# Decode-state streams issued from GpSimd's queue, up to three sequences ahead, in 14 buffers

## The chip, the cores and the metric

The kernel runs on one core of a Trainium2 chip. The metric is device time in microseconds, from runs without a profiler; the median of three is quoted. One further execution was taken with the hardware profiler, and every row below comes from that one.

## The reference, cut to what matters

One inference step of a one-layer decoder trunk, for 512 prompt tokens and, beside them, 8 decode sequences of one token each. In order: a mixer (RG-LRU heads and four mLSTM heads on one input projection), cross-attention of four heads over 256 memory tokens, and a squared-ReLU MLP; each is added to the residual. All arithmetic is fp32.

The decode sequences carry states of their own, and these are what the change is about:

```
# mLSTM, per decode sequence b and head h; C0[b,h] is 256 x 256
C_new = g_state * C + g_in * outer(v, k)          # written out as s_mlstm_C
num   = C_new @ q                                  # then divided by a denominator
# cross-attention, per decode sequence b and head h
s = q . K[b, :, h, :] * 512**-0.5                  # K: 256 memory tokens x 512
p = softmax(s)
o = p @ V[b, :, h, :]                              # V: 256 memory tokens x 512
```

K and V for 8 sequences and 4 heads are 16.8 MB each, C is 8.4 MB. Each is read once, so each is a stream from HBM.

## The kernel before, in words

Activations lie with features on the 128 partitions and 520 columns (512 prompt tokens and 8 decode tokens). A fp32 product is three matmuls: weight and activation are each split into a rounded high part and a low remainder. The whole kernel is one list of jobs. A job is a 512 KB granule of weights: it is loaded into one of three `wraw` buffers (`w_raw`, L103 to 106), split by ScalarE (`whi`, L121) and VectorE (`wlo`, L122), and multiplied on TensorE. `run_jobs` (L140) issues, for job i, the load of job i+3, the split of job i+2, the matmuls of job i, and its eviction. Loads and splits get a priority that moves them 100 instructions forward.

Everything that isn't a weight matmul is a task, a Python generator. `step_tasks` (L129) advances the open tasks once per job (`rate` and `cost` say how many steps), so that a task's instructions are interleaved with the jobs' on the in-order queues of the engines. A task started with a rate takes rate times cost steps a job: `attn_decode_all` has rate 2 (`DRATE`); a job of the projections `w_cq` has cost 1, a job of `w_mk` or `w_mv` cost 0.35 (`MCOST`).

Two tasks stream the decode states.

- `ml_decode(h)` (L442 to 503), once for each of the four mLSTM heads, in the stretch of the input projection. It writes q and k of the 8 sequences to a DRAM tile `dqk`, and then takes four steps of two sequences. A step needs two rows of `dqk`, each broadcast to 128 partitions (256 KB as written to SBUF, L475), and two granules of C (256 KB each, L479). ScalarE scales C (L493), VectorE adds the outer product (L494) and reduces against q (L497), and the new C is stored (L500).
- `attn_decode(h)` (L766 to 821), once a head, in the stretch of the projections `w_cq`, `w_mk` and `w_mv`. Eight steps of one sequence each load a broadcast row of q (L780, 256 KB) and two granules of K (L782, 256 KB each); VectorE multiplies and reduces (L792). After four empty steps come a TensorE transpose (L798), a softmax over 8 rows, and a store of the probabilities to a DRAM tile `dp` (L802). Eight more steps load a broadcast row of p (L806, 128 KB) and two granules of V (L808, 256 KB each), and VectorE reduces four times (L819).

`attn_prompt(h)` waits, as a task, until `attn_decode(h)` is done, before it multiplies by the values.

All DMAs are issued by one queue, SyncE's (`load = nc.sync.dma_start`), in the order that the job list and the tasks give them. That queue is in order: a load that waits for its buffer holds back whatever stands behind it. In the streams, a step starts the loads of the next step, so they run one step ahead. The buffers for K, V and all broadcast rows are one ring of six 2 KB tiles a partition (tag `kv`); granules of C lie in the general pool of 66 slots. GpSimd itself does 15 additions in the prologue, eight small memsets (L551) and 10 multiplications at the end.

Of the kernel before, what the change touches and what calls it, by code (L numbers as in the profile page):

```python
# [9 lines left out]
F32 = mybir.dt.float32  # L10
F32R = mybir.dt.float32r
AF = mybir.ActivationFunctionType
ALU = mybir.AluOpType
# [4 lines left out]
P = 128  # L18
TP = 512
NB = 8  # L20
# [6 lines left out]
NMEM = 256  # L27
# [18 lines left out]
def tile_trunk(ctx: ExitStack, tc: tile.TileContext, a, o):  # L46
    nc = tc.nc
    V, S, PE, G = nc.vector, nc.scalar, nc.tensor, nc.gpsimd
# [8 lines left out]
    small = early_pools.enter_context(tc.tile_pool(name="small", bufs=2))  # L57
# [6 lines left out]
    def nm(s):  # L64
        uid[0] += 1
        return f"{s}_{uid[0]}"

    def slot(name, shape=(P, T), dt=F32):
        return slots.tile(list(shape), dt, tag="slot", name=nm(name))

    def sm(name, shape, bufs=2, dt=F32):
        return small.tile(list(shape), dt, tag=name, name=nm(name), bufs=bufs)

    def stream(shape):
        return small.tile(list(shape), F32, tag="kv", name=nm("kv"), bufs=6)

    def aux():
        return late.get("aux", paux).tile([P, 512], F32, tag="aux", name=nm("aux"))
# [10 lines left out]
    def rows_of(d, off, n):  # L89
        return bass.AP(tensor=d.tensor, offset=d.offset + off, ap=[[0, P], [1, n]])  # L90

    load = nc.sync.dma_start
    HALF = [slice(0, HT), slice(HT, T)]
    DEC = slice(TP, T)
    CH = 128
# [64 lines left out]
    def gemm(srcs, acts, evac, pre=None, cols=(0, 1)):  # L160
# [4 lines left out]
        def mm(g, wh, wl):  # L165
# [3 lines left out]
            for j in range(8):  # L169
                k = g * 8 + j  # L170
                xh, xl = acts[k]
                for wi, (w, x) in enumerate(((wh, xh), (wh, xl), (wl, xh))):
                    for hf in cols:
                        PE.matmul(ps[:, hf, 0:HT], w[:, j, :], x[:, HALF[hf]],  # L174
                                  start=(k == 0 and wi == 0), stop=(k == n - 1 and wi == 2))
# [11 lines left out]
    def pc(base, i=0):  # L187
        return par[:, base + i:base + i + 1]
# [31 lines left out]
    def rstd_of(ssq, n, name):  # L220
        r = slot(name)
        v = slot(name + "v")
        for c in HALF:
            ps = aux()
# [217 lines left out]
    def ml_decode(h, q, k, hh):  # L442

        v = vv[h]
        qkd = sm("qkd", (NB, 512))
        tp = aux()
        for i, s_ in enumerate((q[0], q[1], k[0], k[1])):
            PE.transpose(out=tp[0:NB, i * P:(i + 1) * P], in_=s_[:, DEC], identity=ident)
        S.copy(qkd, tp[0:NB, :])
        dqk = dram.tile([NB, 512], F32, name=nm("dqk"))  # L450
        load(dqk, qkd)
        gv, t1, t2 = sm("gv", (P, 2, NB)), sm("t1", (P, 2, NB)), sm("t2", (P, 2, NB))
        for j in range(2):
            V.tensor_tensor(out=gv[:, j], in0=v[j][:, DEC], in1=bc[:, h, 1], op=ALU.mult)
            V.tensor_tensor(out=t1[:, j], in0=nst[:, h, j], in1=bc[:, h, 0], op=ALU.mult)
            V.tensor_tensor(out=t2[:, j], in0=k[j][:, DEC], in1=bc[:, h, 1], op=ALU.mult)
        V.tensor_tensor(out=t1, in0=t1, in1=t2, op=ALU.add)
        for j in range(2):
            V.tensor_tensor(out=t2[:, j], in0=t1[:, j], in1=q[j][:, DEC], op=ALU.mult)
        yield  # L460
        yield
        load(o["s_n"][:, h], t1)
        dps = aux()
        for j in range(2):
            PE.matmul(dps[:, 0:NB], ones, t2[:, j], start=(j == 0), stop=(j == 1))
        den, numd = sm("den", (P, NB)), sm("numd", (P, 2, NB))
        S.activation(den, dps[:, 0:NB], AF.Abs)
        V.tensor_tensor(out=den, in0=den, in1=bc[:, h, 2], op=ALU.max)
        V.reciprocal(den, den)

        def fetch(b2):
            qb, ct = [], []
            for b in (2 * b2, 2 * b2 + 1):
                t = stream((P, 512))
                load(t, rows_of(dqk, b * 512, 512))  # L475
                qb.append(t)
            for j in range(2):
                t = slot("ct", (P, 2, 256))
                load(t, a["C0"][h, j, :, 2 * b2:2 * b2 + 2])  # L479
                ct.append(t)  # L480
            return qb, ct

        cur = fetch(0)
        for b2 in range(NB // 2):
            yield
            qb, ct = cur
            if b2 + 1 < NB // 2:
                cur = fetch(b2 + 1)
            for j in range(2):
                for i in range(2):  # L490
                    b = 2 * b2 + i
                    c = ct[j][:, i]
                    S.activation(c, c, AF.Copy, scale=bc[:, h, 0, b:b + 1])  # L493
                    V.scalar_tensor_tensor(out=c, in0=qb[i][:, 256:512], scalar=gv[:, j, b:b + 1],  # L494
                                           in1=c, op0=ALU.mult, op1=ALU.add)
                    junk = sm("junk", (P, 256), 1)
                    V.tensor_tensor_reduce(out=junk, in0=c, in1=qb[i][:, 0:256], op0=ALU.mult,  # L497
                                           op1=ALU.add, scale=1.0, scalar=0.0,
                                           accum_out=numd[:, j, b:b + 1])
                load(o["s_C"][h, j, :, 2 * b2:2 * b2 + 2], ct[j])  # L500
        for j in range(2):
            V.tensor_tensor(out=hh[j][:, DEC], in0=numd[:, j], in1=den, op=ALU.mult)
        dec_done[h] = True

    def ml_prompt(h):
# [12 lines left out]
        for i in range(2):  # L518
            out = [slot("qk") for _ in range(2)]
            for j in range(2):  # L520
                for c in HALF:
                    ps = aux()
# [114 lines left out]
    def rnn(i, xc):  # L637
# [5 lines left out]
        for g in range(2):  # L643
            t = slot("g")
            for c in HALF:
                ps2 = aux()
# [104 lines left out]
    def softmax(ps, rows, out):  # L751
        mx = sm("mx", (P, 1), 4)[0:rows]
        su = sm("su", (P, 1), 4)[0:rows]
        V.reduce_max(out=mx, in_=ps, axis=AX.X)
        V.tensor_scalar(out=mx, in0=mx, scalar1=-SC, scalar2=None, op0=ALU.mult)
        S.activation(out, ps, AF.Exp, bias=mx, scale=SC, accum_out=su)
        V.reciprocal(su, su)
        V.tensor_scalar(out=out, in0=out, scalar1=su, scalar2=None, op0=ALU.mult)
# [7 lines left out]
    def attn_decode(h):  # L766
        q = qx[h]
        yield
        tp = aux()
        for j in range(4):  # L770
            PE.transpose(out=tp[0:NB, j * P:(j + 1) * P], in_=q[j][:, DEC], identity=ident)
        qd = sm("qkd", (NB, 512))
        S.copy(qd, tp[0:NB, :])
        dq = dram.tile([NB, 512], F32, name=nm("dq"))
        load(dq, qd)
        sc = sm("sc", (P, 2, NB))

        def fetch(b):
            ts = [stream((P, 512)) for _ in range(3)]
            load(ts[0], rows_of(dq, b * 512, 512))  # L780
            for i in range(2):
                load(ts[1 + i], a["K"][h, b, i])  # L782
            return ts

        cur = fetch(0)
        for b in range(NB):
            yield
            qb, *kt = cur
            if b + 1 < NB:
                cur = fetch(b + 1)  # L790
            for i in range(2):
                V.tensor_tensor_reduce(out=kt[i], in0=kt[i], in1=qb, op0=ALU.mult, op1=ALU.add,  # L792
                                       scale=1.0, scalar=0.0, accum_out=sc[:, i, b:b + 1])
        for _ in range(4):
            yield
        tp = aux()
        for i in range(2):
            PE.transpose(out=tp[0:NB, i * P:(i + 1) * P], in_=sc[:, i], identity=ident)  # L798
        pd = sm("pd", (NB, NMEM))
        softmax(tp[0:NB, 0:NMEM], NB, pd)  # L800
        dp = dram.tile([NB, NMEM], F32, name=nm("dp"))
        load(dp, pd)  # L802

        def fetch(b):
            ts = [stream((P, 512)) for _ in range(3)]
            load(ts[0][:, 0:NMEM], rows_of(dp, b * NMEM, NMEM))  # L806
            for i in range(2):
                load(ts[1 + i].rearrange("p (a b) -> p a b", a=2), a["V"][h, b, i])  # L808
            return ts

        cur = fetch(0)
        for b in range(NB):
            yield
            pb, *vt = cur
            if b + 1 < NB:
                cur = fetch(b + 1)
            for j in range(4):
                t = vt[j // 2][:, (j % 2) * NMEM:(j % 2 + 1) * NMEM]
                V.tensor_tensor_reduce(out=t, in0=t, in1=pb[:, 0:NMEM], op0=ALU.mult, op1=ALU.add,  # L819
                                       scale=1.0, scalar=0.0, accum_out=od[:, 4 * h + j, b:b + 1])  # L820
        adec_done[h] = True

# [182 lines left out]
    def fact_out(x1, n):  # L1005
        fact[n] = [pair_slot("fa") for _ in range(2)]
        for hf in range(2):
            split_to(fact[n][hf], x1[:, HALF[hf]], pc(C_FFN, n))
        i, kp = divmod(n, 2)
# [8 lines left out]
        else:  # L1018
            for hf in range(2):
                S.activation(r[:, 1 - hf], x1[:, HALF[hf]], AF.Copy, scale=pc(C_FFN, n))  # L1020

# [395 lines left out]
```

## Time and profile before

| | |
|---|---|
| median of 3 runs | 2764.72 us (2763.32 to 2767.06) |
| the profiled execution: its time | 2765.53 us |
| the profiled execution: its span | 2763.7 us |
| TensorE busy | 2684.4 us, 97% of the span |
| VectorE / ScalarE / GpSimd busy | 2092.8 / 1213.1 / 31.7 us |
| moved by DMA | 512.39 MB, mean 185 GB/s |

The span is the time from the first to the last instruction of the profiled execution; that execution's own time is 1.8 us more. Busy times overlap, since the engines work side by side. The granted clock is TensorE's: 1.00 is 2.4 GHz, 0.50 is 1.2 GHz.

### The profile page before, as it was taken

What the parts mean: (1) busy time and instruction counts of PE and PEld (TensorE: products, weight loads), DVE (VectorE), ACT (ScalarE), POOL (GpSimd) and SP (SyncE); (2) the same over time, 40 slices, a digit from 0 to 9 for tenths busy, and PEclk for the clock granted to TensorE, in tenths of its full rate; (3) what the DMA queues carried; (4) which work ended last, traced back from release to release, by engine and by line L of the source; (5) the groups of instructions that cost most, each with busy time, mean ns of one, the idle gap of its engine ahead of it and who ended that gap; (6) DMA issues with size and microseconds to landing.
All of it is one profiled execution on the core that took longest, in us unless ns stands there. A gap on an engine that the chain in (4) does not pass through costs nothing.

```text
span 2763.7 us, 52667 instructions
## 1 busy us (share of the span) xinstructions
PE 2684.4 (97%) x21582; PEld 2641.6 (96%) x21582; DVE 2092.8 (76%) x3470; ACT 1213.1 (44%) x1622; POOL 31.7 (1%) x37
## 2 busy tenths in 40 slices
PE   7999999999999989999999999999999999999996
PEld 6999999999999988889999999999999999999995
DVE  7767687753346567774558999999999888989897
ACT  3444455642233124444435555555554333333344
POOL 3000000000000000000000000000000000000001
PEclk9999999999999999999999999999999999999998
DMA  4455452324446787765557656565669766555641
GB/s 151 137 172 169 158 169 84 92 92 133 139 140 207 252 271 234 239 221 169 184 182 240 229 195 209 184 207 192 202 200 334 258 208 219 178 173 178 215 130 70
DMA packets 245386, 512.39 MB, mean 185 GB/s; under 512 B 25516, under 2 KB 97868, under 8 KB 245144
## 3 DMA queue, kind: packets, MB, share of 16 engines
q1 hardware_dynamic: 245144, 509.02, 56.1%
q8 instruction: 170, 2.79, 0.4%
q14 instruction: 72, 0.59, 0.1%
HBM read 416.14 MB, written 92.92 MB: 184 GB/s over the span
## 4 chain that ended last, share of the span: by engine, by line
PE 82%; DMA 8%; DVE 7%; ACT 1%; issue 1%; SPq 1%; DVEq 0%; ACTq 0%
PE mm L1104 45%; PE mm L174 29%; DMA kv<-in_K 3%; DMA kv<-in_V 2%; PE aux L193 2%; PE mm L904 2%; DVE wlo L122 2%; PE mm L875 2%; DMA ct<-in_C 1%; PE mm L1148 1%; DVE kv L819 1%; DVE kv L792 0%; DVE y L1259 0%; DVE xh L311 0%; DVE xl L312 0%
## 5 line engine op out<-in xcount | busy, mean ns | idle before, releaser
L121 ACT CAST whi<-wraw 128x1024 fp32r<-128x1024 f32 x498 | 522.8, 1050 | 1026.4 <-PE mm L1104 420.0
L122 DVE TENSOR_TENSOR wlo<-wraw,whi 128x1024 fp32r<-128x1024 f32 x498 | 609.7, 1225 | 215.0 <-ACT whi L121 213.7
L1104 PE MATMUL mm<-ha,whi 128*128 128x260 f32 x3584 | 643.2, 283 | 0.5 <-DVE X L1212 0.3
L1104 PEld LDWEIGHTS mm<-ha,whi 128*128 128x128 f32 x3584 | 551.1, 188 | 1.1 <-DVE X L1212 0.7
L1104 PE MATMUL mm<-ha,wlo 128*128 128x260 f32 x1792 | 504.7, 282 | 0.0
L1104 PE MATMUL mm<-ta,whi 128*128 128x260 f32 x1984 | 357.3, 282 | 0.0
L1104 PEld LDWEIGHTS mm<-ha,wlo 128*128 128x128 f32 x1792 | 337.0, 188 | 0.0
L1104 PEld LDWEIGHTS mm<-ta,whi 128*128 128x128 f32 x1984 | 303.9, 188 | 0.0
L174 PE MATMUL mm<-xh,whi 128*128 128x260 f32 x1312 | 274.2, 290 | 11.1 <-DVE xh L311 10.8
L1104 PE MATMUL mm<-ta,wlo 128*128 128x260 f32 x992 | 278.7, 281 | 0.0
L174 PE MATMUL mm<-xl,whi 128*128 128x260 f32 x1312 | 268.3, 286 | 5.6 <-DVE xl L312 5.5
L1104 PE MATMUL mm<-fa,whi 128*128 128x260 f32 x1488 | 271.1, 283 | 0.0
L174 PE MATMUL mm<-xh,wlo 128*128 128x260 f32 x1312 | 268.2, 285 | 0.3 <-DVE wlo L122 0.3
L1104 PEld LDWEIGHTS mm<-fa,whi 128*128 128x128 f32 x1488 | 229.2, 188 | 0.0
L174 PEld LDWEIGHTS mm<-xh,whi 128*128 128x128 f32 x1312 | 206.7, 191 | 13.7 <-ACT whi L121 6.5
L174 PEld LDWEIGHTS mm<-xl,whi 128*128 128x128 f32 x1312 | 205.5, 191 | 7.8 <-DVE xl L312 7.8
L1104 PE MATMUL mm<-fa,wlo 128*128 128x260 f32 x744 | 209.8, 282 | 0.0
L174 PEld LDWEIGHTS mm<-xh,wlo 128*128 128x128 f32 x1312 | 205.7, 191 | 0.7 <-DVE wlo L122 0.6
L121 ACT CAST whi<-A 128x1024 fp32r<-128x1024 f32 x126 | 132.2, 1050 | 163.1 <-PE mm L1104 162.9
L1212 DVE TENSOR_TENSOR X<-mm,X 128x260 f32<-128x260 f32 x448 | 170.5, 421 | 41.2 <-PE mm L1104 40.9
L1104 PEld LDWEIGHTS mm<-ta,wlo 128*128 128x128 f32 x992 | 186.6, 188 | 0.0
L122 DVE TENSOR_TENSOR wlo<-A,whi 128x1024 fp32r<-128x1024 f32 x126 | 153.9, 1221 | 13.7 <-ACT whi L121 13.6
(371 smaller groups left out, 4854.8 us busy)
## 6 DMA issues: line engine op xcount, KB each, us to landing
ha<-hc SPq DMA_DIRECT2D x224, 260.0 KB
wraw<-in_w_in SPq DMA_DIRECT2D x80, 512.0 KB
wraw<-in_w_up SPq DMA_DIRECT2D x66, 512.0 KB
A<-in_w_down SPq DMA_DIRECT2D x64, 512.0 KB
wraw<-in_w_down SPq DMA_DIRECT2D x64, 512.0 KB
A<-in_w_up SPq DMA_DIRECT2D x62, 512.0 KB
hc<-hhi SPq DMA_DIRECT2D x32, 910.0 KB
hc<-r SPq DMA_DIRECT2D x32, 910.0 KB
```

The costliest lines, as they stand in the source:

```text
L121: S.copy(hi, raw)
L122: V.tensor_tensor(out=lo, in0=raw, in1=hi.bitcast(F32), op=ALU.subtract)
L174: PE.matmul(ps[:, hf, 0:HT], w[:, j, :], x[:, HALF[hf]], start=(k == 0 and wi == 0), stop=(k == n - 1 and wi == 2))
L193: PE.matmul(out, u, v, start=first and i == 0, stop=last and i == 2)
L819: V.tensor_tensor_reduce(out=t, in0=t, in1=pb[:, 0:NMEM], op0=ALU.mult, op1=ALU.add, scale=1.0, scalar=0.0, accum_out=od[:, 4 * h + j, b:b ...
L875: PE.matmul(box["ps"], w[:, i, :], x, start=(k == 0 and wi == 0), stop=(k == KB - 1 and wi == 2))
L904: PE.matmul(box["ps"][:, i], x[:, ms], w[:, j], start=(k == 0 and wi == 0), stop=(k == KB - 1 and wi == 2))
L1104: PE.matmul(out, w[:, j, :], x[:, b], start=(new and k == 0 and wi == 0), stop=(p == LAST[acc] and k == per - 1 and wi == 2), skip_group_c ...
L1148: PE.matmul(ps[:, hf, 0:HT], w[:, j, :], x[hf][:, b], start=(kp == 0 and j == 0 and wi == 0), stop=(kp == 1 and j == 7 and wi == 2))
L1212: V.tensor_tensor(out=x, in0=c, in1=x, op=ALU.add)
```

## The change

The loads of K, V, C, of the rows of q, k and p move from SyncE's queue to GpSimd's (`stream_load = nc.gpsimd.dma_start`). All other DMAs, the stores of q, k and p to DRAM included, stay where they are. The ring `kv` has 14 buffers in place of six. In `ml_decode` two steps are fetched ahead in place of one. In `attn_decode` three sequences are fetched ahead, for K and for V; K's granules are issued ahead of the row of q; the first three sequences of V are issued right behind the steps of K, ahead of the softmax; the rows of p are loaded for two sequences by one DMA (256 KB), 16 in all in place of 32.

```diff
-        return small.tile(list(shape), F32, tag="kv", name=nm("kv"), bufs=6)
+        return small.tile(list(shape), F32, tag="kv", name=nm("kv"), bufs=14)
...
     load = nc.sync.dma_start
+
+    stream_load = nc.gpsimd.dma_start
...
                 t = stream((P, 512))
-                load(t, rows_of(dqk, b * 512, 512))
+                stream_load(t, rows_of(dqk, b * 512, 512))
                 qb.append(t)
             for j in range(2):
                 t = slot("ct", (P, 2, 256))
-                load(t, a["C0"][h, j, :, 2 * b2:2 * b2 + 2])
+                stream_load(t, a["C0"][h, j, :, 2 * b2:2 * b2 + 2])
                 ct.append(t)
             return qb, ct
 
-        cur = fetch(0)
+        ahead = [fetch(0), fetch(1)]
         for b2 in range(NB // 2):
             yield
-            qb, ct = cur
-            if b2 + 1 < NB // 2:
-                cur = fetch(b2 + 1)
+            qb, ct = ahead.pop(0)
+            if b2 + 2 < NB // 2:
+                ahead.append(fetch(b2 + 2))
...
             ts = [stream((P, 512)) for _ in range(3)]
-            load(ts[0], rows_of(dq, b * 512, 512))
             for i in range(2):
-                load(ts[1 + i], a["K"][h, b, i])
+                stream_load(ts[1 + i], a["K"][h, b, i])
+            stream_load(ts[0], rows_of(dq, b * 512, 512))
             return ts
 
-        cur = fetch(0)
+        ahead = [fetch(b) for b in range(3)]
         for b in range(NB):
             yield
-            qb, *kt = cur
-            if b + 1 < NB:
-                cur = fetch(b + 1)
+            qb, *kt = ahead.pop(0)
+            if b + 3 < NB:
+                ahead.append(fetch(b + 3))
...
+        def fetch_v(b):
+            ts = [stream((P, 512)) for _ in range(2)]
+            for i in range(2):
+                stream_load(ts[i].rearrange("p (a b) -> p a b", a=2), a["V"][h, b, i])
+            return ts
+
+        ahead = [fetch_v(b) for b in range(3)]
         for _ in range(4):
             yield
...
-        cur = fetch(0)
+        pbs = []
+
+        def fetch_p(b2):
+            t = stream((P, 2, NMEM))
+            stream_load(t, rows_of(dp, 2 * b2 * NMEM, 2 * NMEM).rearrange("p (a b) -> p a b", a=2))
+            pbs.append(t)
+
+        fetch_p(0)
+        fetch_p(1)
         for b in range(NB):
             yield
-            pb, *vt = cur
-            if b + 1 < NB:
-                cur = fetch(b + 1)
+            vt = ahead.pop(0)
+            if b % 2 == 0 and 4 <= b + 4 < NB:
+                fetch_p(b // 2 + 2)
+            if b + 3 < NB:
+                ahead.append(fetch_v(b + 3))
+            pb = pbs[b // 2][:, b % 2]
             for j in range(4):
                 t = vt[j // 2][:, (j % 2) * NMEM:(j % 2 + 1) * NMEM]
-                V.tensor_tensor_reduce(out=t, in0=t, in1=pb[:, 0:NMEM], op0=ALU.mult, op1=ALU.add,
+                V.tensor_tensor_reduce(out=t, in0=t, in1=pb, op0=ALU.mult, op1=ALU.add,
```

## Rows read from the trace of the kernel before

**Rows 1.** Busy time by engine, whole span: us, share, instructions.
```profile
PE 2684.4 (97%) x21582; PEld 2641.6 (96%) x21582; DVE 2092.8 (76%) x3470; ACT 1213.1 (44%) x1622; POOL 31.7 (1%) x37
```
**Rows 2.** Stretches: busy us of each engine, granted clock, DMA share, GB/s.
```profile
core 0: us, PE busy (x) PEld busy (x) DVE busy (x) ACT busy (x) POOL busy (x), PEclk, DMA share, GB/s
100.00:430.00 330.00, 319.17 (x2541) 313.00 (x2541) 239.11 (x613) 170.45 (x310) 0.81 (x8) 0.98 0.51 159
430.00:850.00 420.00, 420.00 (x3474) 418.81 (x3473) 224.97 (x319) 169.94 (x223) 0.00 (x0) 1.00 0.37 116
850.00:950.00 100.00, 99.51 (x828) 98.72 (x828) 62.06 (x172) 27.10 (x39) 0.00 (x0) 1.00 0.78 254
950.00:1260.00 310.00, 287.23 (x1848) 258.54 (x1847) 206.46 (x526) 125.04 (x216) 0.00 (x0) 0.96 0.73 238
1260.00:2734.00 1474.00, 1473.46 (x12307) 1472.71 (x12306) 1259.30 (x1681) 676.04 (x776) 0.00 (x0) 1.00 0.60 199
```
**Rows 3.** Waits of PE, 100 to 430 us: total us, times, longest.
```profile
PE aux L193 <- DVE C L584: 4.7, 2, 2.6
PE aux L193 <- ACT qk L526: 4.5, 1, 4.5
```
**Rows 4.** Waits of ScalarE for the stream of C, 100 to 430 us.
```profile
ACT ct L493 <- DMA ct<-in_C: 44.2, 11, 6.0
```
**Rows 5.** Chain that ended last, 150 to 172 us: start, us, what.
```profile
155.15 7.09 DMA ct<-in_C
...
162.27 1.71 ACT ct L493 x4
...
170.53 1.67 PE aux L193 x6
```
**Rows 6.** Waits of PE, 850 to 1260 us.
```profile
PE mm L875 <- DVE wlo L122: 5.0, 3, 2.9
PE aux L193 <- ACT qah L202: 4.0, 1, 4.0
...
PE aux L193 <- ACT mvh L202: 3.0, 2, 2.8
```
**Rows 7.** Waits of VectorE and ScalarE for DMAs, 850 to 1260 us.
```profile
DVE kv L792 <- DMA kv<-in_K: 49.2, 21, 5.3
DVE kv L819 <- DMA kv<-in_V: 35.0, 27, 3.0
...
ACT whi L121 <- DMA wraw<-in_w_mk: 15.3, 5, 6.3
```
**Rows 8.** Three short stretches, columns as in Rows 2.
```profile
1000.00:1010.00 10.00, 6.69 (x54) 6.28 (x53) 6.45 (x14) 2.10 (x2) 0.00 (x0) 1.00 0.94 319
...
1030.00:1040.00 10.00, 5.86 (x18) 4.08 (x17) 6.92 (x12) 3.92 (x7) 0.00 (x0) 0.70 0.68 223
...
1250.00:1260.00 10.00, 8.50 (x35) 7.03 (x36) 5.24 (x11) 4.70 (x11) 0.00 (x0) 0.83 0.71 256
```
**Rows 9.** Chain that ended last: a stretch of w_in jobs, one of w_mk jobs.
```profile
428.06 23.00 PE mm L174 x192
...
1139.36 19.91 PE mm L875 x168
```
**Rows 10.** Waits of SyncE's queue for the streams, 850 to 1260 us.
```profile
SPq L780 <- DVE sc L792: 17.3, 10, 3.0
...
SPq L782 <- DVE sc L792: 6.1, 11, 1.3
```
**Rows 11.** Tile kv: count, duration ns min/median/max, first and last start us.
```profile
L819 DVE CUSTOM_DVE_ANT_0 kv<-kv,kv x128: 406/420/428, 897.4 to 1207.1; 128x256 f32<-128x256 f32 x128
...
L782 SPq DMA_DIRECT2D kv<-in_K x64: 327/425/1342, 857.1 to 1137.5; - x64
```
**Rows 12.** GpSimd by line: count, busy us, mean ns, idle before.
```profile
L326 POOL TENSOR_TENSOR ssq<-ssq,x 128x520 f32<-128x520 f32 x15 | 21.8, 1453 | 24.2 <-ACT x L325 23.8
```
**Rows 13.** VectorE by line and shape, 850 to 1260 us: columns as in Rows 12.
```profile
L758 DVE TENSOR_SCALAR p<-p,su 128x256 f32<-128x256 f32 x16 | 5.6, 352 | 0.4
```

More of the change, by code (lines that the diff above doesn't have):

```diff
@@ L802, in attn_decode @@
         load(dp, pd)
[L804 to L809, printed above, removed]
-        cur = fetch(0)
+        pbs = []
[5 more added lines that the diff above has]
+        fetch_p(1)
         for b in range(NB):
             yield
-            pb, *vt = cur
-            if b + 1 < NB:
-                cur = fetch(b + 1)
+            vt = ahead.pop(0)
[4 more added lines that the diff above has]
+            pb = pbs[b // 2][:, b % 2]
             for j in range(4):
                 t = vt[j // 2][:, (j % 2) * NMEM:(j % 2 + 1) * NMEM]
-                V.tensor_tensor_reduce(out=t, in0=t, in1=pb[:, 0:NMEM], op0=ALU.mult, op1=ALU.add,
+                V.tensor_tensor_reduce(out=t, in0=t, in1=pb, op0=ALU.mult, op1=ALU.add,
                                        scale=1.0, scalar=0.0, accum_out=od[:, 4 * h + j, b:b + 1])
```

## The prediction

> **What bounds the kernel now.** I read the busy times first: TensorE is busy for 97% of the span [rows 1], so a change to loads can only win the time in which TensorE stands still, or runs at half clock. The windows by stage come next [rows 2]. TensorE never idles from 430 to 850 us, and hardly from 1260 to 2734 us. Of 100 to 430 us, where C is streamed, it idles 330 - 319.2 = 10.8 us. From 850 to 1260 us, where K and V are streamed, it idles 0.5 + 22.8 = 23.3 us. The granted clock adds to this. It is 0.98 and 0.96 in the first and last of these three stretches, a mix of the levels 2.4 and 1.2 GHz, and a stretch at half clock does half the work: 0.02 x 330 = 6 us and 0.04 x 310 = 12 us. So the ceiling is about 17 us in C's stage and 36 us in the attention's, 53 us together. Prologue and tail have no stream in them.
>
> Are the streams what TensorE stands still for? It never waits for one directly; they sit two engines back. In C's stage its two largest waits are for results of VectorE and ScalarE [rows 3]; ScalarE had stood 44.2 us in 11 waits for C [rows 4], and the chain shows the order: 7.09 us of C's DMA, ScalarE's scaling, some work of both engines, TensorE's next matmul [rows 5]. These engines are in order, so a scaling that waits for C holds back the splits and copies behind it. In the attention's stage TensorE waits for `wlo` and for other splits [rows 6], and VectorE had stood 49.2 us for K and 35.0 us for V [rows 7]. One case isn't the streams': the stall of 2.8 us for ScalarE's split of values [rows 6] falls at the stage's end, where from 1250 to 1260 us TensorE idles 1.5 us and the clock is 0.83 [rows 8], 40 us after the last stream instruction [rows 11]. It and its half-clock loss, 0.17 x 10 = 1.7 us, take 4.5 us off that ceiling and leave 31.5.
>
> **The change, part by part.**
>
> *C two steps ahead.* The mean wait is 44.2 / 11 = 4.0 us, the longest 6.0 [rows 4]. One more step of lead is one job, and 192 matmuls, four jobs, take 23.0 us [rows 9]: 5.75 us. So most waits should end, except at each head's first step, whose load starts as late as now, save that it stands no longer behind SyncE's other loads. The stage isn't short of bandwidth (159 GB/s on average, DMA share 0.51 [rows 2]). Between nothing and the 17 us I take 11, about two thirds: three steps of four get more lead, and a shorter stall may also spare its stretch at half clock.
>
> *K and V three sequences ahead.* The waits average 49.2 / 21 = 2.3 and 35.0 / 27 = 1.3 us [rows 7], and two sequences of lead are more than that. What limits the gain is bytes. A `w_mk` job is 19.91 x 24 / 168 = 2.84 us of TensorE [rows 9] and needs 524 KB of weights. The decode task takes 2 x 0.35 = 0.7 sequences a job, each with 786 KB for K and its row, 655 KB for V and its row: 550 or 459 KB. Together 1074 or 983 KB a job; at 319 GB/s, the rate of the fullest 10 us shown [rows 8], that takes 3.37 or 3.08 us, 0.53 or 0.24 us more than the matmuls. Eight sequences take 11.4 jobs, so two heads in this stretch lose 2 x 11.4 x (0.53 + 0.24) = 17.5 us to bandwidth, whoever issues the loads. The attention's own matmuls give some of it back, and weights are waited for already now, 15.3 us of `w_mk` [rows 7]. So of 31.5 I take 14.
>
> *SyncE's queue loses the streams.* Seven kinds of wait for buffers, rows and probabilities, 17.3 to 6.1 us each, sum to 67.6 us [rows 10], and weight loads stand behind them. They go to GpSimd's queue, where nothing stands behind them but other stream loads and the eight memsets of `tn`. Late next is then the weight load itself, for its buffer or for bandwidth. I book nothing extra: it is within the 14, since a weight load that starts early still shares the DMA engines.
>
> *K ahead of the row of q; V ahead of the softmax; p for two sequences.* Each head's first K and V need no longer wait for the DRAM round trip. On GpSimd the row of q waits for the store of q, and behind it the next K waits; what the first sequence needs is issued already. The DMAs for p halve in number, their bytes stay. Counted in the 14.
>
> *Issuing on GpSimd.* The trace has no DMA from this queue, so its price is bounded. Below by SyncE's issue, 0.43 us [rows 11]; above by the longest work of GpSimd in the trace, 1.45 us for an addition over 520 columns [rows 12]. I take the upper one. The attention issues 4 x (16 + 8 + 16 + 4) = 176 loads between 857 and 1207 us [rows 11], one per 1.99 us, so 176 x 1.45 = 255 us fit into 350. The 64 loads of the C stage (93 us of 330) fit too. GpSimd is idle there, and that idleness is the cover; without it each load would cost its issue time.
>
> *Slots and buffers.* Two more steps of C hold two more slots of 66. The pool is shared with everything else in the stage, and TensorE's waits there are for results, not for room [rows 3], so I take 0; if a missing slot held one job a head, 4 x 5.75 = 23 us is the upper end.
>
> *VectorE beside GpSimd.* The trace shows 16 scalings of p at 0.35 us, 5.6 us in all, from 850 to 1260 us [rows 13]; if every one stood still for one issue of GpSimd, VectorE would lose 16 x 1.45 = 23 us, but spread out, and VectorE is idle for 141 of those 410 us [rows 2]. I take 0. The Trainium skill, "SBUF — State Buffer", section "Who interferes with whom", speaks against the change here: descriptors of GpSimd's DMAs are written through an SBUF port pair that VectorE's two-port copies and scalings lock, and either blocks the other. By it these 16 instructions are the ones in question, and the sum would be lower by at most part of the 23 us; no row of this trace shows such a block.
>
> **The sum.** 11 + 14 = 25 us off 2765.5, the profiled execution's own time (span 2763.7 and 1.8 around it): 2740.5. The median lies 0.8 us below that execution: 2740.
>
> **The rivals.**
>
> *The bytes decide (no change).* All loads keep sharing the DMA engines, and two queues full at once halve what a weight load gets: at half of 319 GB/s, 524 KB take 3.3 us against 2.84 us of matmuls. For: DMA share 0.94 at 319 GB/s just where TensorE idles 3.3 us in 10 [rows 8], and the waits for `w_mk`. Against: another such place has only 0.68 and 223 GB/s [rows 8], and the stage averages 0.73 to 0.78 [rows 2]. Then the attention wins nothing and C's stage 5 to 6 us: 2759, within 2754 to 2766. The rule in "DMA: Bandwidth & Descriptors" of the Trainium skill, section "Issuing engines are not separate DMA queues", is this rival: loads of several queues run on the same DMA engines, and a second queue saves only issue time. The rows so far bear out half of it, since bandwidth is short in some windows alone.
>
> *GpSimd issues too slowly (slower).* A load costs more than the 1.99 us that the attention has for each. Place: the queue's order; VectorE then waits for every sequence, and TensorE for `wlo`. Price: 176 x (cost - 1.99); at 2.2 us 37 us, at 2.5 us 90 us, less the 11 of C's stage: 2790 to 2845. From 2.1 us on it outweighs C's gain. For: nothing in the trace tells the cost. Against: it is well beyond both rows taken as bounds. A milder form, below 1.99 us on average but late in the bursts of three sequences, ends at 2766 to 2785.
>
> *The loads start no earlier.* GpSimd's queue is in order too. If a row of q or p, waiting for its store, or a memset holds the loads behind it, lead is lost at each head's start, eight times about 5 us of VectorE's waiting. What is left of the gain is then that of the middle steps, about half: 2752.
>
> **How the numbers follow.** This measurement can tell about 0.2% (5.5 us) from no change. Forecast, 2716 to 2750: 0.52. Late starts, 2750 to 2756: 0.10. Bytes decide: 0.19, of which 0.05 below 2759.2 and 0.14 within 0.2%. GpSimd too slow or other stalls: 0.19. Faster is 0.52 + 0.10 + 0.05 = 0.67, same 0.14, slower 0.19. The low end is nearly the full ceiling, 2765 - 49 = 2716. The high end takes in the rival of bytes and the milder form of the slow queue: 2780.
>
> **What would show it.** Right: VectorE's waits for K and V fall from 84 us below 30 and ScalarE's for C from 44 below 15; TensorE's idle time in C's stage falls to about 4 us and from 850 us to the end of the attention to 12 to 15; fewer stretches at half clock; GpSimd's loads take 0.4 to 1.5 us each. Wrong: waits for `wraw` grow by as much as those for K and V fall (bytes), GpSimd's queue is full from 857 us on (issue), or the time that TensorE wins before 1260 us is lost behind it.

## The result, and the profile after

The changed kernel takes 2736.6 us (median of four runs, 2736.3 to 2740.7) against 2764.0 us (2758.8 to 2767.1) for the kernel before on the same chip: a ratio of 0.9903, 95% interval 0.9891 to 0.9914. That is 27 us faster, and 2740 was forecast. The profiled execution took 2736.3 us, its span 2734.6.

Line numbers have moved by a few: `wlo` is L124 now, `whi` L123, a `w_mk` matmul L888, K's reduction L794, V's L832, C's scaling L495. First the busy times, as in [rows 1]:

```profile
PE 2671.2 (98%) x21582; PEld 2630.8 (96%) x21582; DVE 2093.0 (77%) x3470; ACT 1215.6 (44%) x1624; POOL 160.7 (6%) x277
```

GpSimd has 240 loads more to issue, and VectorE's busy time is what it was. Then the stretches, cut as in [rows 2], with the later ones moved by the time won (busy us of each engine, granted clock, DMA share, GB/s):

```profile
core 0: us, PE busy (x) PEld busy (x) DVE busy (x) ACT busy (x) POOL busy (x), PEclk, DMA share, GB/s
100.00:430.00 330.00, 327.18 (x2647) 321.40 (x2648) 249.72 (x629) 178.41 (x322) 36.33 (x74) 1.00 0.50 165
430.00:850.00 420.00, 420.00 (x3478) 418.68 (x3477) 223.00 (x319) 168.80 (x224) 4.46 (x9) 1.00 0.38 118
850.00:950.00 100.00, 98.65 (x824) 98.21 (x823) 61.29 (x173) 27.16 (x34) 37.62 (x71) 1.00 0.79 275
950.00:1230.00 280.00, 266.06 (x1735) 238.88 (x1734) 197.79 (x511) 120.82 (x211) 51.49 (x96) 0.99 0.72 245
1230.00:2704.00 1474.00, 1473.21 (x12313) 1472.36 (x12313) 1260.34 (x1682) 675.75 (x777) 0.00 (x0) 1.00 0.60 199
```

TensorE's idle time in C's stage fell from 10.8 us to 330 - 327.2 = 2.8, in the attention's from 23.3 us to 1.35 + 13.94 = 15.3: eight us in each. The rest of the 29 us of span is clock: it was 0.98 and 0.96 and is now 1.00 and 0.99, so the loss to half speed fell from 6.6 + 12.4 to 0.01 x 280 = 2.8 us, read from two digits and so coarse. Outside prologue and tail the trace of before has eight half-clock stretches, 34 us long in all; after has two, at 1042 and 1107 us, 3.4 us each, and TensorE had stood still 2.5 and 2.0 us right ahead of them. By that list the clock gave 17.0 - 3.4 = 13.6 us, and with the 16 us of idle time that is the 29.

Who waits now? First C's stage, 100 to 430 us (engine and line, for what: total us, times, longest), where [rows 3, 4] showed 4.7 and 4.5 for TensorE and 44.2 for ScalarE:

```profile
PE aux L649 <- DVE C L586: 1.6, 1, 1.6
PE aux L195 <- DVE C L586: 0.9, 1, 0.9
...
ACT ct L495 <- DMA ct<-in_C: 14.9, 6, 4.0
```

Then the attention's stage, 840 to 1235 us, which answers to [rows 6, 7]:

```profile
DVE kv L794 <- DMA kv<-dq: 20.5, 15, 3.3
...
ACT whi L123 <- DMA wraw<-in_w_mk: 17.2, 7, 7.3
...
DVE kv L832 <- DMA kv<-dp: 10.2, 4, 3.7
...
PE aux L195 <- ACT mvh L204: 7.3, 3, 2.8
...
ACT whi L123 <- DMA wraw<-in_w_mv: 3.5, 3, 1.7
...
PE mm L888 <- DVE wlo L124: 2.7, 2, 2.4
```

K and V themselves are hardly waited for any more: 0.9 us of V, where it was 49.2 and 35.0 us for both. What VectorE waits for are the rows of q and p (`dq`, `dp`). ScalarE waits for the weights of `w_mk` slightly longer than before, 17.2 us against 15.3. Its waits for all weights of the stage became shorter all the same, 20.7 us against 31.0, since the kernel before had these two as well:

```profile
ACT whi L121 <- DMA wraw<-in_w_cq: 13.1, 2, 7.4
...
ACT whi L121 <- DMA wraw<-in_w_mv: 2.6, 2, 2.1
```

GpSimd by line (count, busy us, mean ns, idle before) answers to [rows 12]:

```profile
L783 POOL DMA_DIRECT2D kv<-in_K x64 | 34.4, 538 | 23.6 <-DMA kv<-dq 5.6 <-DMA kv<-in_K 5.0 <-issue 2.3
L800 POOL DMA_DIRECT2D kv<-in_V x64 | 34.4, 538 | 26.4 <-DMA kv<-dp 5.2 <-DMA kv<-in_K 4.5 <-DVE od L832 4.0
...
L784 POOL DMA_DIRECT2D kv<-dq x32 | 17.2, 538 | 539.3 <-DMA dq<-qkd 500.8 <-DVE qal L205 32.9 <-DMA kv<-in_K 2.0
L481 POOL DMA_DIRECT2D ct<-in_C x32 | 17.2, 537 | 59.7 <-DVE numd L499 23.6 <-issue 18.2 <-DMA kv<-dqk 8.4
```

A load costs GpSimd 0.54 us, whatever it reads.

### The profile page after: what moved, and what is told of

Same layout as the page of the kernel before. It is cut to its first block, busy times and chain, and to the rows that moved or that the text cites. A ratio compares the mean times of both kernels' runs of the same rounds, so it can differ in the third digit from the quotient of the medians.

```text
span 2734.6 us, 52765 instructions
## 1 busy us (share of the span) xinstructions
PE 2671.2 (98%) x21582; PEld 2630.8 (96%) x21582; DVE 2093.0 (77%) x3470; ACT 1215.6 (44%) x1624; POOL 160.7 (6%) x277
## 4 chain that ended last, share of the span: by engine, by line
PE 89%; DVE 5%; DMA 3%; issue 1%; ACT 1%; POOL 0%; DVEq 0%; SPq 0%; ACTq 0%; POOLq 0%
PE mm L1117 45%; PE mm L176 35%; PE mm L888 2%; PE aux L195 2%; PE mm L917 1%; DVE wlo L124 1%; PE mm L1161 1%; DMA kv<-dq 1%; DMA wraw<-in_w_mk 1%; PE aux L649 1%; ACT whi L123 0%; DVE y L1272 0%; DVE xh L313 0%; DVE xl L314 0%; PE aux L578 0%
## 5 line engine op out<-in xcount | busy, mean ns | idle before, releaser
L123 ACT CAST whi<-wraw 128x1024 fp32r<-128x1024 f32 x498 | 522.9, 1050 | 1027.6 <-PE mm L1117 422.4
L124 DVE TENSOR_TENSOR wlo<-wraw,whi 128x1024 fp32r<-128x1024 f32 x498 | 610.6, 1226 | 227.4 <-ACT whi L123 225.5
L123 ACT CAST whi<-A 128x1024 fp32r<-128x1024 f32 x126 | 132.4, 1051 | 163.1 <-PE mm L1117 159.1
L124 DVE TENSOR_TENSOR wlo<-A,whi 128x1024 fp32r<-128x1024 f32 x126 | 154.0, 1222 | 13.4 <-ACT whi L123 13.3
```

The costliest lines, as they stand in the source:

```text
L123: S.copy(hi, raw)
L124: V.tensor_tensor(out=lo, in0=raw, in1=hi.bitcast(F32), op=ALU.subtract)
```

## The experiments

The forecast was met, but a sum can come out right with wrong terms. The change has three parts: 14 buffers, more lead, another queue. (A fourth, the new order of the loads in the attention, goes with the lead in every run and was not tried apart.) So the runs take them apart, first by stage, then by queue. All were timed in three rounds; the kernel before took 2764.9 us beside the first four, 2766.4 beside the next four (e5 to e8) and 2760.9 beside the last four.

The last two columns are worked out from the traces: the starts of the n-th matmul in the two profiled executions are compared, here and in the kernel before; "C" is the difference reached at 850 us, "attention" what is added by 1300 us. One execution each, so a few us of scatter must be allowed for: nine runs share the code of C's stage (the change, e3, e5, e7 to e12), and their C lies between -11.6 and -14.6.

| run | median us | ratio, 95% interval | C | attention |
|---|---|---|---|---|
| the change | 2736.6 | 0.9903 (0.9891 to 0.9914) | -12.5 | -15.8 |
| e1: queue alone | 2795.4 | 1.0113 (1.0089 to 1.0137) | +3.4 | +27.8 |
| e2: buffers and lead, all on SyncE | 2728.0 | 0.9864 (0.9841 to 0.9886) | -6.9 | -27.0 |
| e3: C's part alone, 14 buffers | 2735.1 | 0.9893 (0.9873 to 0.9913) | -14.6 | -15.5 |
| e4: attention's part alone, 14 buffers | 2746.6 | 0.9936 (0.9916 to 0.9957) | -5.4 | -11.3 |
| e5: C on GpSimd, K and V on SyncE | 2723.3 | 0.9846 (0.9832 to 0.9861) | -13.6 | -25.5 |
| e6: 14 buffers alone | 2748.1 | 0.9931 (0.9915 to 0.9948) | -1.5 | -12.7 |
| e7: the change, attention's weights on GpSimd too | 2730.4 | 0.9873 (0.9858 to 0.9888) | -12.2 | -24.3 |
| e8: as e5, attention's weights on GpSimd | 2730.9 | 0.9872 (0.9857 to 0.9886) | -13.8 | -20.6 |
| e9: the change, fourth raw buffer | 2731.2 | 0.9890 (0.9873 to 0.9906) | -11.6 | -22.0 |
| e10: e5 with fourth raw buffer | 2720.1 | 0.9847 (0.9832 to 0.9861) | -13.4 | -30.8 |
| e11: the change, rows of q and p on SyncE | 2732.4 | 0.9891 (0.9877 to 0.9906) | -11.8 | -19.1 |
| e12: the change, 12 buffers | 2737.1 | 0.9907 (0.9891 to 0.9922) | -11.9 | -16.1 |

**e1, the queue alone.** The kernel before, its six stream loads issued by GpSimd; six buffers, one step of lead.

```diff
+    stream_load = nc.gpsimd.dma_start
...
-                load(t, a["C0"][h, j, :, 2 * b2:2 * b2 + 2])
+                stream_load(t, a["C0"][h, j, :, 2 * b2:2 * b2 + 2])
...
-                load(ts[1 + i], a["K"][h, b, i])
+                stream_load(ts[1 + i], a["K"][h, b, i])
```

> Only the queue changes: the six kinds of stream load go to GpSimd's queue, with six buffers, one step of lead and the old order of loads. Theory A (lead: the waits ended because the loads start two steps earlier; the queue only makes room): VectorE still waits over 60 us for K, V and their rows and ScalarE over 30 us for C, gain 4 to 8 us of the 27, about 2758 us. Theory B (queue: the loads stood behind SyncE's other work): those waits fall by more than half and most of the gain is there, 2740 to 2746 us.

It was 31 us slower, nearly all of it in the attention; neither theory had allowed for a loss. Waits of VectorE and ScalarE there, 850 to 1260 us:

```profile
DVE kv L820 <- DMA kv<-in_V: 50.4, 24, 6.0
DVE kv L793 <- DMA kv<-in_K: 49.5, 27, 4.0
...
ACT whi L122 <- DMA wraw<-in_w_mk: 31.0, 8, 8.1
ACT whi L122 <- DMA wraw<-in_w_cq: 8.5, 1, 8.5
```

The streams come no earlier for the other queue (49.5 and 50.4 us against 49.2 and 35.0), and the weights of `w_mk` are waited for twice as long (31.0 us against 15.3). So moving to a second queue is, with six buffers, no gain in itself; in the attention it is a loss. In C's stage ScalarE's wait for C fell from 44.2 to 26.5 us, and yet 3.4 us were lost: the sum of an engine's waits is not a price.

**e2, buffers and lead without the queue.** The changed kernel with one line put back:

```diff
-    stream_load = nc.gpsimd.dma_start
+    stream_load = nc.sync.dma_start
```

> The whole change, except that the stream loads stay on SyncE's queue (14 buffers, two or three sequences ahead, the new order). Theory A (lead): most of the gain is kept, 2738 to 2746 us. Theory B (queue): the loads stand behind weight loads that wait for a buffer, and weight loads behind stream loads that wait for one, so that little is gained or time is lost: 2758 to 2775 us, with SyncE's waits for the streams over the 68 us of before.

It is 10 us faster than theory A expected at best. The attention wins 27.0 us in place of 15.8, C's stage 6.9 in place of 12.5. The stretch from 850 to 1260 us:

```profile
850.00:1260.00 410.00, 403.28 (x2899) 376.66 (x2898) 275.50 (x706) 158.39 (x261) 0.00 (x0) 1.00 0.74 250
```

TensorE idles 6.7 us and the clock is whole, with every byte moved that the changed kernel moves. In C's stage, 100 to 430 us, ScalarE still waits 32.8 us for C, and SyncE's queue shows what C's loads stand behind. L502 is the store of the new C, which waits for VectorE:

```profile
ACT ct L495 <- DMA ct<-in_C: 32.8, 7, 5.9
...
SPq L502 <- DVE ct L496: 48.7, 19, 5.0
SPq L502 <- DVE numd L499: 22.5, 11, 3.5
```

**e3, C's part alone.** The kernel before with 14 buffers, C and its rows on GpSimd's queue, two steps ahead.

```diff
-                load(t, a["C0"][h, j, :, 2 * b2:2 * b2 + 2])
+                stream_load(t, a["C0"][h, j, :, 2 * b2:2 * b2 + 2])
...
-        cur = fetch(0)
+        ahead = [fetch(0), fetch(1)]
```

> Only C's part of the change (C and its rows on GpSimd's queue, two steps ahead, 14 buffers); K and V as before. If the two stages are independent, as the shift of TensorE's work between the two traces says (12.5 us by 850 us, 16 to 17 us more by 1260 us), this gains 12 to 13 us: 2751 to 2752 us. If the C stage's gain came from fewer loads on SyncE alone or were given back later, under 8 us: above 2756 us.

C's stage wins 14.6 us, ScalarE's wait for C is 13.5 us. That the attention wins 15.5 us too, with its code as before, was the surprise: only the ring is larger.

**e4, the attention's part alone.** The changed kernel with C's loads back on SyncE's queue, one step ahead.

```diff
-                stream_load(t, a["C0"][h, j, :, 2 * b2:2 * b2 + 2])
+                load(t, a["C0"][h, j, :, 2 * b2:2 * b2 + 2])
...
-        ahead = [fetch(0), fetch(1)]
+        cur = fetch(0)
```

> Only the attention's part (K, V and their rows on GpSimd's queue, three sequences ahead, p for two sequences, 14 buffers); C on GpSimd's queue too, but one step ahead. If the C stage's gain came from its second step of lead (theory A), what is left is the attention's 16 to 17 us: 2747 to 2749 us. If the C stage's gain came from the other queue (theory B), this kernel is as fast as the full change: 2736 to 2739 us.

The expectation says that C stays on GpSimd's queue; the run has it on SyncE's, so that queue and second step are both gone, and the run can't tell theory A from theory B. The attention wins 11.3 us: with all of its part, no more than e3 had without it. The change has the same code there and 15.8: the scatter of single traces, or the stages acting on each other.

**e5, each stream on the queue that suited it.** C and its rows on GpSimd's queue, K, V and their rows on SyncE's.

```diff
-    stream_load = nc.gpsimd.dma_start
+    stream_load = nc.sync.dma_start
+    c_load = nc.gpsimd.dma_start
...
-                stream_load(t, a["C0"][h, j, :, 2 * b2:2 * b2 + 2])
+                c_load(t, a["C0"][h, j, :, 2 * b2:2 * b2 + 2])
```

> The full change, but only C and its rows go to GpSimd's queue; K, V and their rows stay on SyncE's, three sequences ahead. If what each queue gave in each stage of the runs so far adds up (C on GpSimd two steps ahead 12 to 14 us; K and V on SyncE three ahead 27 us), the gain is 39 to 41 us: 2723 to 2726 us, the fastest so far. If the stages act on each other, it stays at 2728 or above.

The two stages add up as expected: 2723.3 us, 0.9846 of before. It beats both kernels.

**e6, the buffers alone.**

```diff
-        return small.tile(list(shape), F32, tag="kv", name=nm("kv"), bufs=6)
+        return small.tile(list(shape), F32, tag="kv", name=nm("kv"), bufs=14)
```

> The kernel before with 14 buffers in place of six, nothing else. Theory A (lead): more buffers alone start no load earlier, since one step is fetched ahead: within 5 us of before, 2760 to 2767 us. Theory C (buffers: with six, a step's loads wait on SyncE's queue for the buffers of the step in work, and weight loads stand behind them): the attention's 15 us that C's part alone showed came from the buffers, so 2747 to 2752 us, and SyncE's 68 us of waits for the streams are nearly gone.

One number wins 18.3 us against the kernel before on its chip, two thirds of the change's 27, and 14.2 by the trace, 12.7 of it in the attention. SyncE's queue shows why; its waits from 850 to 1260 us:

```profile
SPq L806 <- DVE od L819: 0.8, 2, 0.6
SPq L808 <- DVE od L819: 0.4, 1, 0.4
SPq L782 <- DVE sc L792: 0.3, 1, 0.3
...
SPq L780 <- DVE sc L792: 0.2, 1, 0.2
```

These are the waits for a buffer that VectorE still reads; L780's was 17.3 us, L782's 6.1 [rows 10]. (Waits for the stores of q and p, 7.1 and 7.2 us, stay.) With six buffers, three to a step, a step's loads could not be issued until the step in work had given back its own, and on an in-order queue the weight loads stood behind them: ScalarE's wait for `w_mk` is 6.1 us here and was 15.3 [rows 7].

**e7, weights and streams together on GpSimd's queue**, and **e8, the two swapped** (e5 with the attention's weights on GpSimd). They tell whether GpSimd's queue is slow in itself or whether it is the splitting that costs. The edit of both:

```diff
+    n_attn = len(jobs)
...
+    for j in jobs[n_attn:]:
+        j["put"] = nc.gpsimd.dma_start
...
-        load(raw, src)
+        (put or load)(raw, src)
```

> The full change, and the weight loads of w_cq, w_mk and w_mv go to GpSimd's queue as well, so that in the attention's stage weights and streams stand in one queue again. Theory D (two queues share the DMA engines, and weights lose what the order of one queue gave them): ScalarE's waits for w_mk fall from 17 us below 8, and the attention gains 22 to 28 us in place of 16: 2724 to 2731 us. Theory E (loads issued by GpSimd are slower by themselves): no better than the full change, 2736 us or above, with those waits at 17 us or more.

> The queues of the attention's stage exchanged: weights of w_cq, w_mk and w_mv on GpSimd's queue, K, V and their rows on SyncE's, three ahead; C on GpSimd's as in the full change. Theory D (sharing between two queues): about as the full change, 2733 to 2740 us, since the weights again share with the streams. Theory E (GpSimd's path slow by itself): worse than the full change, over 2742 us, since now the weights, with less lead, take that path.

By the traces, the attention wins 24.3 us on one queue, GpSimd's, much as on SyncE's (25.5 and 27.0); split the other way round it wins 20.6. Two comparisons by time say that splitting costs: the change against e7, which differ in the queue of the weights alone (ratios 0.9903 and 0.9873, intervals apart), and e8 against e5, 7.6 us on the same chip, though e8 is faster than either theory expected.

But by the medians e7 is no faster than e8 (2730.4 and 2730.9 us) and 7.1 us slower than e5, and the execution that was profiled is the fastest of e7's four. So that GpSimd's queue costs nothing by itself is not shown: between e5 and e7 it costs 1 us of the attention by the traces and 7 us by the medians.

What is late when there are two? In the runs with deep buffers, K and V on GpSimd's queue and the weights on SyncE's (the change, e4, e12) two waits stand out against the runs with one queue (e2, e5, e7): the rows of p, 9 to 10 us against 3 to 5, and `w_mk`, 10 to 17 against 3 to 8 (e8 lies between, with 5.5 and 9.6). The same two lines in e5, 840 to 1235 us:

```profile
DVE kv L833 <- DMA kv<-dp: 3.6, 4, 1.6
...
ACT whi L124 <- DMA wraw<-in_w_mk: 7.0, 4, 2.8
```

ScalarE's waits for all weights together do not separate the runs: 13.3 us in e12, 20.2 in e4 and 20.7 in the change against 13.7 to 15.5. The chain of work that ended last does. From 850 to 1230 us, `w_mk` loads are on it for 14 to 20 us in the change, e4, e8, e11 and e12, and for 5 us at most in e2, e5 and e7. The last four runs try the remedies.

**e9, weights a job earlier, with e12 as its control, and e10, the same in e5.** A fourth buffer of raw weights for every fourth job of the attention, at the price of two of the 14; e12 has 12 buffers and nothing else.

```diff
-        return small.tile(list(shape), F32, tag="kv", name=nm("kv"), bufs=14)
+        return small.tile(list(shape), F32, tag="kv", name=nm("kv"), bufs=12)
...
-        raw = wpool.tile([P, 8, P], F32, tag="wraw", name=nm("wraw"))
+        raw = (small.tile([P, 8, P], F32, tag="wraw4", name=nm("wraw4"), bufs=1) if fourth else
+               wpool.tile([P, 8, P], F32, tag="wraw", name=nm("wraw")))
...
+    for j in jobs[n_attn + 3:n_early:4]:
+        j["fourth"] = True
```

> The changed kernel, with a fourth buffer for raw weights in the attention's stage (every fourth job there takes it), paid for by two buffers of kv (12 in place of 14); streams stay on GpSimd's queue. In the trace of the changed kernel SyncE's queue stands 186 us for wlo before it may load the next weights, so a weight load starts one job and not more before its split. Theory W (the two queues cost time because weights, started that late, must compete with the bursts of streams): one more job of lead covers it; ScalarE's waits for w_mk fall from 17 to under 7 us, and of the 11 us lost to the second queue 7 to 11 come back: 2725 to 2730. Theory R (what is late are the rows of q and p, which stand on GpSimd's queue behind the granules of K and V): weights earlier change little, 2733 to 2739. Theory B (bytes decide, every load that comes earlier pushes another back): no gain, 2735 to 2742, VectorE's waits for kv grow by what ScalarE's fall.

> The same fourth raw buffer and 12 buffers of kv, in the version with only C on GpSimd's queue and K, V and their rows on SyncE's (2723). Theory W: with one queue the weights are not late (ScalarE's waits for w_mk 7 us), so little is left to win: 2719 to 2724. If the fourth buffer wins as much here as in the two-queue version, it is worth something by itself and says nothing on the queues.

> The changed kernel with 12 buffers of kv in place of 14, and nothing else: the control for the two runs with a fourth raw buffer. K's streams hold 4 x 3 = 12 buffers with three sequences ahead, V's 4 x 2 and two or three rows of p, so little should change: 2734 to 2740. If fewer buffers hold the bursts back and that helps the weights, 2728 to 2733.

Twelve buffers do as well as 14, though ScalarE waits 10.5 us for `w_mk` in place of 17.2. Against that control the fourth raw buffer wins 5.9 us in the two-queue version, by the trace as well as by the medians, though the intervals of the two ratios overlap. The waits of ScalarE for weights in e9, 840 to 1235 us:

```profile
ACT whi L124 <- DMA wraw<-in_w_mk: 5.2, 1, 5.2
ACT whi L124 <- DMA wraw<-in_w_mv: 0.7, 1, 0.7
```

But e10, on the same chip, is still 11.1 us faster than e9: the gap between one queue and two, 13.3 us without the buffer (the change and e5, on different chips), is nearly as wide. Whether e10 gains on e5 is unclear: by the trace its attention is 5.3 us ahead, by the ratios to the kernel before they are the same. So late weights cost something in the two-queue version: with the fourth buffer no weight load is on the chain any more, and 5.9 us came back where theory W expected 7 to 11. They are not all that separates the versions; as the whole cause theory W fails.

**e11, the rows of q and p back on SyncE's queue.**

```diff
-            stream_load(ts[0], rows_of(dq, b * 512, 512))
+            load(ts[0], rows_of(dq, b * 512, 512))
...
-            stream_load(t, rows_of(dp, 2 * b2 * NMEM, 2 * NMEM).rearrange("p (a b) -> p a b", a=2))
+            load(t, rows_of(dp, 2 * b2 * NMEM, 2 * NMEM).rearrange("p (a b) -> p a b", a=2))
```

> The changed kernel, with only the rows of q and p in the attention back on SyncE's queue; K and V stay on GpSimd's. Theory R: VectorE's waits for the rows (20.5 and 10.2 us) fall, for p's to about 3, and 5 to 11 us come back: 2726 to 2731. Theory W: the rows now stand on SyncE's queue among the weights and wait there for their buffers, the weights behind them; no gain or a few us lost: 2735 to 2742.

Waits for DMAs in the same stretch of e11:

```profile
ACT whi L123 <- DMA wraw<-in_w_mk: 17.8, 5, 7.9
...
DVE kv L794 <- DMA kv<-dq: 16.9, 12, 3.3
DVE kv L832 <- DMA kv<-dp: 4.0, 4, 1.2
```

The rows of p come in time (4.0 us for 10.2), and the run is 4.7 us faster than e12 on the same chip, by the trace 3.3 us ahead of the change; the intervals of the ratios overlap. That is just short of what theory R expected. By the trace, rows that stand behind granules of K and V on one queue are then about a third of the loss, though 3 us is within the scatter; the weights are as late as ever.

## Why the prediction was right, and where it was not

**C's stage: right in size, half right in its reason.** 11 us were forecast of a ceiling of 17; 12.5 came, ScalarE's wait fell to 14.9 us (below 15 was named) and TensorE idles 2.8 us (about 4). But the 11 us were booked for the second step of lead, and "no longer behind SyncE's other loads" was named for each head's first step alone. On SyncE's queue the same lead and ring win 6.9 (e2), of which the ring alone may be 1.5 (e6) to 5.4 (e4); with the other queue as well it is 11.6 to 14.6 in nine runs, so the queue gave 4.7 to 7.7 us. The queue without the lead, and with six buffers, wins nothing (e1). The step that was left out is that the loads of the second step would stand on SyncE's queue behind the stores of C, which wait 71 us there in e2.

**The attention: right in sum, wrong in its terms.** 14 us were forecast and 15.8 came. Two steps of the working failed, and that they cancelled was luck.

*"= 17.5 us to bandwidth, whoever issues the loads."* That went by 319 GB/s, the fullest ten microseconds I had shown [rows 8], taken for a ceiling. It was none, and the trace of the kernel before could have told: a stretch of its MLP, then two of the changed kernel's attention (columns as in [rows 2]):

```profile
2091.00:2101.00 10.00, 9.66 (x81) 9.45 (x80) 9.65 (x15) 6.05 (x6) 0.00 (x0) 1.00 1.05 404
```
```profile
980.00:990.00 10.00, 7.65 (x65) 7.44 (x64) 6.62 (x18) 3.15 (x3) 5.48 (x12) 1.00 1.03 393
...
1090.00:1100.00 10.00, 9.53 (x43) 7.32 (x42) 10.00 (x29) 4.19 (x10) 4.82 (x9) 1.00 1.03 390
```

At 390 GB/s, estimated from these rows, the 1074 KB of a job take 2.75 us, less than its 2.84 us of matmuls: by that rate the term is 0 and not 17.5. The same bytes are moved in e2, e5 and e10, which win 27.0, 25.5 and 30.8 us, the last nearly all of the 31.5 that were named as the ceiling.

*"SyncE's queue loses the streams"* and *"I book nothing extra"*. The waits of [rows 10] were half of the matter: 14 buffers alone, which end them, win 12.7 to 15.5 us (e6, e3), and no other queue is needed for it. More lead on that one queue, with the new order of the loads, wins some 10 to 14 us beyond (e2 and e5 against e3 and e6). The second queue, whose cost the sum held at nothing, then takes 10 to 11 us of it (the change against e5 and e2). What is left of the change in the attention is what its ring alone would have won.

**The second queue's cost, as far as it is settled.** It is not GpSimd's issue (0.54 us a load), and by the traces hardly its path (e7; the medians leave up to 7 us open). It shows in two places, rows of p behind granules, about a third (e11), and weights that land late (e9), of which the fourth buffer takes away 6 us but takes away as much or none in the one-queue version. In the changed kernel's trace both can be seen. First the start of a head; GpSimd from 968 us on, after it had waited for the store of q:

```profile
968.10 0.54 POOL L784 DMA_DIRECT2D kv<-dq  x1 [8.81 <-DMA dq<-qkd]
968.65 1.16 POOL L783 DMA_DIRECT2D kv<-in_K  x2
969.87 0.54 POOL L784 DMA_DIRECT2D kv<-dq  x1
970.49 1.15 POOL L783 DMA_DIRECT2D kv<-in_K  x2
```

It goes on so to 986 us, 22 loads in 18 us; from 975 us SyncE issues three `w_mk` loads, and the DMAs are full (the ten microseconds from 980 us above). TensorE stands still for 2.35 us until 988.9, and the chain (start, us, what) shows for which row:

```profile
979.48 4.97 DMA kv<-dq
984.45 0.60 DVE kv L794
...
987.72 1.14 DVE wlo L124
```

VectorE stood for a row of q (and then 1.3 us for nothing that the profile names), and the `wlo` that TensorE needs came behind the reductions that these rows feed. ScalarE stands 3.0 us for weights at the same time, but for a split that TensorE needs two jobs later; in e5 it stands 2.8 us there, and TensorE stands still for less than 0.3. In the next stand-still, 2.5 us at 1040 us, row and weights are one chain:

```profile
1025.47 4.88 DMA kv<-dp
...
1031.96 1.14 DVE wlo L124
...
1033.12 6.58 DMA wraw<-in_w_mk
...
1039.79 1.04 ACT whi L123
```

A row of p holds VectorE, its `wlo` gives the buffer of raw weights back late, and the next weight load, which may start only then, takes 6.58 us (7.49 ahead of the stand-still at 1104 us); TensorE goes on when ScalarE's split and copies behind that load are done. On one queue a weight load's turn comes between two granules by the order of the program. That this order is the cause is argued, not shown: no run held the streams on the second queue back to the pace of the first, and rows and weights together weren't mended in one run. That part stays open.

**The other steps.** GpSimd's issue was taken at 1.45 us between 0.43 and 1.45; it is 0.54, and the rival *GpSimd issues too slowly* is dead. *Slots* and *VectorE beside GpSimd* were taken at 0 and are 0: VectorE's busy time is 2093.0 us against 2092.8, and the 16 scalings of p took 355 ns against 352 [rows 13]. Nine of the 16 ran beside an issue of GpSimd; of these one took 397 ns, the others 344 to 358. The block that the Trainium skill ("SBUF — State Buffer", "Who interferes with whom") speaks of does not show here beyond that one. *The loads start no earlier* is dead for K and V, and lives in what is left of the wait for C, six waits in 14.9 us, and in the rows. *The bytes decide* is refuted as a limit on the gain by e2 and e5, which move the same bytes; its other half, that two queues at once slow a weight load, is what the late `w_mk` loads of the split runs look like. The rule that stood beside that rival (the Trainium skill, "DMA: Bandwidth & Descriptors", "Issuing engines are not separate DMA queues") says that a second queue saves issue time alone. In the attention that is not enough, since the second queue cost time. In C's stage the second queue saved 4.7 to 7.7 us; whether that is more than issue time is not shown, since 64 loads at 0.43 us are 27 us of SyncE's queue.

Of the signs named, VectorE's waits for K and V fell from 84 to 0.9 us (below 30 was named), but 30.7 us of waits for their rows took their place; TensorE's idle time in the attention fell to 15.3 (12 to 15). The wrong sign, waits for `wraw` that grow as those for K and V fall, did not show: 17.2 against 15.3 for `w_mk`, 20.7 against 31.0 for all weights.

## What to carry to other kernels

When an in-order queue waits for a stream's buffers, give the stream more buffers before you give it a queue: one number won half or more of what this change won, and in the attention lead on the same queue won more than lead on a second one. The second queue paid for C, whose loads had stood behind other waits of SyncE's queue, and cost for K, V and the weights, probably because the order of one queue had kept both on time. For a ceiling of bandwidth, search the whole trace and not the stage in question: the fullest window of a stage whose queue waits is no ceiling.

## What the runs showed of the hardware that was not expected

- In the attention the changed kernel moved 390 to 393 GB/s over ten microseconds, at a DMA share of 1.03, where [rows 8] had shown 319; the MLP of the kernel before reached 404 at 1.05.
- An issue on GpSimd took 0.536 us at least and in the median, and at most 0.553 us for loads of K, alike for a contiguous granule and a broadcast row; SyncE's took 0.327 to 1.342 us, median 0.425 [rows 11].
- Its loads also go out in larger packets. The page's DMA queues (queue: packets, MB, share of 16 engines), where q0 is GpSimd's and holds 240 loads of 262 KB, 62.9 MB:

```profile
q1 hardware_dynamic: 208280, 446.08, 49.4%
q0 software_dynamic: 19200, 62.93, 6.6%
```

  That is 3278 bytes a packet against 2142 for all else. In e2, where the same 240 loads are on q1, that queue has 242840 packets for 509.01 MB: the 240 loads took 34560 packets there, 1821 bytes each, in place of 19200. Bytes for a share are about the same: 9.5 MB for a per cent on q0, 9.0 on q1.
- Half-clock stretches followed stand-stills of TensorE of 2.0 and 2.5 us in the changed kernel, but not every one as long: after 2.35 us at 987 us and 2.81 us at 1222 us the clock stayed at 1.00.
